# Two transformer blocks on one core: 17 of 22 gate/up pairs of the first block as seven half-size products

## The chip, the core and the metric

The kernel runs on one core of a Trainium2 chip. TensorE (PE) multiplies matrices into PSUM; VectorE (DVE), ScalarE (ACT) and GpSimd (POOL) do the elementwise work; SyncE (SP) only issues transfers between HBM and SBUF. The engines run side by side, each in its own fixed order, and wait for each other on semaphores. The metric is the device time of one execution in microseconds (us).

## The reference, cut to what matters

Two blocks follow each other: 512 positions, width 1024, all in float32. Each is an attention mix and a gated MLP. The change lies in the MLP of the first block:

```
h = rms_norm(x, ln_pre_ffn)                                # 512 x 1024
f = (silu(h @ w_gate) * (h @ w_up)) @ w_down               # w_gate, w_up: 1024 x 2816
x = x + rms_norm(f, ln_post_ffn)
```

## The kernel before

Activations lie transposed in SBUF, as eight tiles of 128 features by 512 positions, and so do the results. To keep float32 accuracy on TensorE, every operand is held as two numbers of a shorter format, hi (the rounded value) and lo (the rest), and every product takes three matmuls: hi·hi, hi·lo and lo·hi (`mm3`). For a weight, `wunit` loads 512 KB (two half units of 128 x 512), ScalarE writes each half's hi (L164) and VectorE its lo (L167). There are two raw buffers (`raw`, two of them in the pool `wts`), and ten of hi and ten of lo. For an activation `split` does the same (L176 to L181).

In `ffn1`, output rows come in 22 pairs, 128 of gate and 128 of up. Each slab is eight blocks of the contraction times three matmuls of 512 columns, so a pair is 48 of them. The normalisation's factor 1/rms per position, R, is applied behind the product: g·R, silu, u·R, their product, and a split into hi and lo, which `w_down` reads (`post`). The first four slabs run side by side (`beside`) in halves of 256 columns, while VectorE still finishes the last stage of the mix in `post`: x is added up, multiplied by `ln_pre_ffn` and split into `h`. R is made behind that (L234 to L236).

A scheduler with a model of the chip sets the order of the instructions on each engine when the kernel is built. All transfers here stand in SyncE's queue in that order, and one that waits for its buffer holds back those behind it.

Of the kernel before, what the change touches and what calls it, by code (L numbers as in the profile page):

```python
# [21 lines left out]
EPS = 1e-6  # L22
BIG = 1e30
WH = 524
# [5 lines left out]
NW = 10  # L30
# [13 lines left out]
KA2 = 6  # L44
BESIDE = 4
NA2 = 4
SLOTS = dict(h=16, o=14, k=16, z=6, v=8, p=8, t=6, m=8)
# [14 lines left out]
class Builder:  # L62
# [120 lines left out]

    def mm3(self, out, ahi, alo, bhi, blo, start, stop):
        mm = self.nc.tensor.matmul
        mm(out, lhsT=ahi, rhs=bhi, start=start, stop=False)  # L186
        mm(out, lhsT=ahi, rhs=blo, start=False, stop=False)  # L187
        mm(out, lhsT=alo, rhs=bhi, start=False, stop=stop)  # L188

# [230 lines left out]
    def setup(self):  # L420
        nc = self.nc
        self.res = None
        self.special = []
        self.mark = None
# [15 lines left out]

    def load_x(self, ks=range(KD)):
        x = []
        for k in ks:
            t = self.slot("v")
            self.load_late(t, self.io["x"][k])
            x.append(t)
        return x
# [89 lines left out]
    def pool_branch(self, us, oT):  # L537
        nc = self.nc
        io = self.io
        add = ALU.add  # L540
        hi, lo = self.wunit("w_pool", 0, 1)[0]
# [6 lines left out]
        for i in range(2):  # L548
            u = us[i]
# [14 lines left out]
            oT[i] = self.split(ps, self.col("pool_scale", i), tag="k")  # L564

    def post(self, a, order, wname, gname, nname, rows):
        nc = self.nc
# [19 lines left out]
        if x is None:  # L587
            x = self.load_x()
        self.res = x
        h = self.h_tiles()  # L590
        gate = None
# [23 lines left out]

    def h_tiles(self):
        return [(self.slot("h", F32R), self.slot("h", F32R)) for _ in range(KD)]

# [10 lines left out]
    def ffn1(self, h, R):  # L629
        nc = self.nc  # L630
        self.tables("silu_and_others")
        get = self.units("w_gu1")
        act = []
        for i in range(KF):
            if i == 0:
# [18 lines left out]
        return self.post(act, None, "w_down", "ln_post_ffn", "ln_mix_2", False)  # L654

    def mix2(self, h, rc):
# [418 lines left out]
```

## Time and profile before

| | |
|---|---|
| median of 3 runs (lowest to highest) | 1339.58 us (1339.52 to 1343.4) |
| the profiled execution | 1343.58 us, span 1341.5 us |
| PE, DVE, ACT, POOL busy, share of the span | 98%, 63%, 50%, 11% |
| mean granted TensorE clock | 0.994 |

The span runs from the first to the last instruction. Busy time is the time in which an engine has an instruction in it. Matmuls overlap in their pipeline: one that "lasts" 0.4 us is followed by the next after 0.23 us, so what it costs is read from the distance of starts. The same holds for VectorE and ScalarE, to a smaller degree.

### The profile page before, as it was taken

The page shows a single profiled execution, that of the slowest core. Times are in us where ns is not written, and L with a number is a line of the kernel's source. Part 1 is how long each engine was busy: PE and PEld are TensorE (multiplying, and loading weights), DVE is VectorE, ACT ScalarE, POOL GpSimd, SP SyncE. Part 2 cuts the span into 40 slices and gives each one's busy share as a digit, 9 for nine tenths or more (in the row PEclk, how much of TensorE's full clock was granted, in tenths as well). Part 3 has the DMA queues.
Part 4 walks back from the last instruction along what each step waited for, and adds up shares of the span by engine and source line. Part 5 has one row for each costly group of instructions (what it writes and reads, how often), then busy time and mean ns, then how long its engine had stood idle before and what let it go on. Part 6 is the DMA issues. An engine that isn't in the chain of part 4 may idle for free.

```text
span 1341.5 us, 20064 instructions
## 1 busy us (share of the span) xinstructions
PE 1311.8 (98%) x7450; PEld 1138.0 (85%) x7450; DVE 851.3 (63%) x1771; ACT 672.6 (50%) x1327; POOL 153.8 (11%) x190
## 2 busy tenths in 40 slices
PE   9799999999999999999999999899999999999998
PEld 9799988988888888888988999779888888888887
DVE  7777885864444432229588878766877777733354
ACT  6466755543333332237576777755554444522241
POOL 1232220000000000001222334430000000000000
PEclk9999999999999999999999999999999999999999
DMA  6322334233333333228244445333332332332221
GB/s 228 109 67 68 95 111 126 70 117 96 96 95 95 94 95 94 95 70 262 88 112 117 123 117 138 93 106 124 126 95 95 94 95 94 102 95 94 94 79 63
DMA packets 48801, 141.69 MB, mean 106 GB/s; under 512 B 6240, under 2 KB 7136, under 8 KB 48704
## 3 DMA queue, kind: packets, MB, share of 16 engines
q1 hardware_dynamic: 48704, 140.42, 34.0%
q8 instruction: 58, 0.95, 0.3%
q14 instruction: 39, 0.32, 0.1%
HBM read 122.38 MB, written 6.29 MB: 96 GB/s over the span
## 4 chain that ended last, share of the span: by engine, by line
PE 84%; DVE 8%; DMA 3%; ACT 2%; issue 2%; SPq 1%; POOL 0%; DVEq 0%; ACTq 0%; POOLq 0%
PE p L186 21%; PE p L187 21%; PE p L188 21%; PE p L372 4%; PE p L373 4%; PE p L374 4%; DVE wl L167 2%; PE p L283 2%; PE p L292 1%; PE p L291 1%; PE p L261 1%; DVE sp L265 1%; PE p L262 1%; DMA wr<-in_w_qk 1%; ACT sp L112 1%
## 5 line engine op out<-in xcount | busy, mean ns | idle before, releaser
L164 ACT ACTIVATE wh<-wr 128x512 fp32r<-128x512 f32 x417 | 259.2, 630 | 405.4 <-PE p L187 351.9
L167 DVE TENSOR_TENSOR wl<-wr,wh 128x512 fp32r<-128x512 f32 (+1 forms) x400 | 286.2, 723 | 238.5 <-ACT wh L164 227.1
L188 PE MATMUL p<-sh,wl 128*128 128x512 f32 (+1 forms) x858 | 320.4, 377 | 0.0
L187 PE MATMUL p<-sh,wh 128*128 128x512 f32 (+1 forms) x858 | 319.5, 376 | 0.1
L186 PE MATMUL p<-sh,wh 128*128 128x512 f32 (+1 forms) x858 | 311.0, 375 | 1.0 <-ACT sh L179 0.7
L372 PE MATMUL p<-wh,sh 128*128 128x256 f32 (+1 forms) x672 | 193.3, 289 | 5.8 <-ACT sz L485 3.3
L373 PE MATMUL p<-wl,sh 128*128 128x256 f32 (+1 forms) x672 | 192.1, 287 | 0.3 <-DVE wl L167 0.2
L374 PE MATMUL p<-wh,sh 128*128 128x256 f32 (+1 forms) x672 | 191.2, 286 | 0.0
L187 PEld LDWEIGHTS p<-sh,wh 128*128 128x128 f32 x858 | 161.2, 188 | 32.6 <-issue 0.5
L188 PEld LDWEIGHTS p<-sh,wl 128*128 128x128 f32 x858 | 161.2, 188 | 31.8 <-issue 0.7
L186 PEld LDWEIGHTS p<-sh,wh 128*128 128x128 f32 x858 | 157.2, 188 | 33.4 <-ACT sh L179 1.1
L372 PEld LDWEIGHTS p<-wh,sh 128*128 128x128 f32 x672 | 128.7, 192 | 9.1 <-ACT sz L485 3.6
L373 PEld LDWEIGHTS p<-wl,sh 128*128 128x128 f32 x672 | 128.9, 192 | 1.1 <-DVE wl L167 0.8
L374 PEld LDWEIGHTS p<-wh,sh 128*128 128x128 f32 x672 | 128.6, 192 | 1.1 <-issue 0.5
L273 POOL TENSOR_SCALAR sp<-sp,m 128x128 f32<-128x128 f32 (+1 forms) x112 | 72.0, 647 | 186.3 <-DVE m L269 145.5
L112 ACT ACTIVATE sp<-sp,m 128x128 f32<-128x128 f32 (+3 forms) x128 | 71.5, 560 | 36.4 <-DVE m L265 33.8
L188 PE MATMUL p<-so,wl 128*128 128x512 f32 (+1 forms) x246 | 88.5, 360 | 0.0
L187 PE MATMUL p<-so,wh 128*128 128x512 f32 (+1 forms) x246 | 88.5, 360 | 0.0
L186 PE MATMUL p<-so,wh 128*128 128x512 f32 (+1 forms) x246 | 87.6, 361 | 0.6 <-DVE m L265 0.5
L167 POOL TENSOR_TENSOR wl<-wr,wh 128x512 fp32r<-128x512 f32 (+1 forms) x17 | 23.8, 1402 | 455.3 <-ACT wh L164 443.7
L265 DVE CUSTOM_DVE_ANT_0 sp<-p,sm 128x128 f32<-128x128 f32 (+3 forms) x128 | 60.4, 483 | 17.3 <-PE p L262 13.5
L187 PE MATMUL p<-sk,wh 128*128 128x512 f32 (+1 forms) x184 | 67.1, 365 | 0.0
(205 smaller groups left out, 2138.8 us busy)
## 6 DMA issues: line engine op xcount, KB each, us to landing
wr<-in_w_gu SPq DMA_DIRECT2D x88, 512.0 KB
wr<-in_w_down SPq DMA_DIRECT2D x44, 512.0 KB
wr<-in_w_qk SPq DMA_DIRECT2D x31, 512.0 KB
sk<-sk SPq DMA_DIRECT2D x88, 128.0 KB
wr<-in_w_out SPq DMA_DIRECT2D x12, 512.0 KB
sv<-in_x SPq DMA_DIRECT2D x16, 256.0 KB
wr<-in_w_ple_gate SPq DMA_DIRECT2D x8, 512.0 KB
wr<-in_w_v SPq DMA_DIRECT2D x6, 512.0 KB
```

What stands on the lines that cost most here:

```text
L112: i = self.nc.scalar.activation(out, in_, func, **k)
L164: nc.scalar.activation(hi[:, :w], c, AF.Copy)
L167: eng.tensor_tensor(lo[:, :w], c, hi[:, :w].bitcast(F32), ALU.subtract)
L186: mm(out, lhsT=ahi, rhs=bhi, start=start, stop=False)
L187: mm(out, lhsT=ahi, rhs=blo, start=False, stop=False)
L188: mm(out, lhsT=alo, rhs=bhi, start=False, stop=stop)
L265: nc.vector.tensor_tensor_reduce(p[:, :n], ps[:, :n], tab[:, (3 - qb) * P:S], 1.0, 3e38, ALU.add, ALU.min, accum_out=m[:, 0:1])
L273: self.nc.gpsimd.tensor_scalar(p[:, :n], p[:, :n], m[:, 2:3], 1.0, ALU.mult, ALU.mult)
L283: ins = nc.tensor.transpose(pt[:, w:w + P], ps_list[qb][:, kb * P:kb * P + P], self.ident)
L372: mm(d, lhsT=h[k][0][:, a], rhs=hi[:, c], start=k == 0 and (o == 0 or not first), stop=False)
L373: mm(d, lhsT=h[k][0][:, a], rhs=lo[:, c], start=False, stop=False)
L374: mm(d, lhsT=h[k][1][:, a], rhs=hi[:, c], start=False, stop=k == 7 and (o > 0 or not first))
```

## The change

Five pairs stay as they were. For the 17 others, the product is cut into blocks: the weights of a pair into gate and up (128 outputs each) by the first and second half of the contraction, the activation into the two halves of the contraction by two halves of the positions. A plain product of two such 2 x 2 block matrices takes eight block products; in the new form (one level of Strassen) it takes seven, with sums of blocks as operands. Each block product is four blocks of the contraction times three matmuls of 256 columns, so a pair is 84 of them.

- The activation's seven operands (28 tiles of hi and lo) are made once: `h_forms` multiplies x by `ln_pre_ffn` and R (`normed`, 16 instructions of 128 x 256), adds and subtracts quarters (8 instructions of 128 x 512) and splits (14 pairs of instructions). The scheduler is given them between the first five pairs. R is now in the operands, not behind the product.
- The weights' seven operands are made for each pair in `w_forms`: both units of the pair are loaded at once, four sums are formed on VectorE, and each of the seven operands is split into hi (ScalarE) and lo (VectorE). The two raw buffers and the numbers of hi and lo buffers are the same.
- Three PSUM tiles A, B, C take the seven products of a pair. Products 5 and 6 run behind the start of the next pair. Copies, additions, silu and multiplications work on 256 columns.
- To free slots, x goes to a tensor in HBM (`parked`, eight stores of 256 KB), and is loaded back for `post`; `act`, `h` and the pool branch's output use other slots.

```diff
     def ffn1(self, h, R):
...
+        self.parked = self.dp.tile([KD, P, S], F32, tag="parked", name="parked")
+        for m in range(KD):
+            nc.sync.dma_start(self.parked[m], self.res[m])
         act = []
-        for i in range(KF):
+        todo = []
+        for i in range(PLAIN):
...
-            act.append(self.split(t, **self.act_tiles(i)))
+            act.append(self.split(t, **self.act_tiles1(i)))
+            if i == 0:
+                forms, todo = self.h_forms(R)
+                each = -(-len(todo) // (PLAIN - 2))
+            else:
+                for step in todo[(i - 1) * each:i * each]:
+                    step()
+        self.res = None
+        sums = [self.slot("m") for _ in range(4)]
+        late = []
+        for i in range(PLAIN, KF):
+            wf = self.w_forms(2 * i, sums)
+            A, B, C = (self.psum(True) for _ in range(3))
+            half = slice(0, 256)
+            e, f, t = self.slot("z"), self.slot("z"), self.slot("z")
+
+            def times(out, j, first=False, wf=wf):
+                hi, lo = wf(j)
+                for k in range(4):
+                    c = slice(k * P, k * P + P)
+                    a = slice(k % 2 * 256, k % 2 * 256 + 256)
+                    bh, bl = forms[j][k // 2]
+                    self.mm3(out[:, half], hi[:, c], lo[:, c], bh[:, a], bl[:, a], first and k == 0, k == 3, True)
+
+            times(A, 0, True)
+            nc.scalar.activation(e[:, half], A[:, half], AF.Copy)
+            times(C, 1, True)
+            for step in late[:1]:
+                step()
+            times(A, 2)
+            nc.scalar.activation(e[:, 256:], A[:, half], AF.Copy)
+            for step in late[1:]:
+                step()
+            times(B, 3, True)
+            nc.vector.tensor_tensor(t[:, half], B[:, half], e[:, half], ALU.add)
+            self.act(t[:, half], t[:, half], AF.Silu)
+            times(A, 4)
+            nc.scalar.activation(f[:, half], A[:, half], AF.Copy)
+            nc.vector.tensor_tensor(f[:, 256:], C[:, half], f[:, half], ALU.add)
+
+            def left(A=A, t=t, times=times):
+                times(A, 5)
+                nc.vector.tensor_tensor(t[:, half], t[:, half], A[:, half], ALU.mult)
+
+            def right(C=C, t=t, e=e, f=f, times=times, i=i):
+                times(C, 6)
+                nc.vector.tensor_tensor(t[:, 256:], C[:, half], e[:, 256:], ALU.add)
+                self.act(t[:, 256:], t[:, 256:], AF.Silu)
+                nc.vector.tensor_tensor(t[:, 256:], t[:, 256:], f[:, 256:], ALU.mult)
+                act.append(self.split(t, -1.0, **self.act_tiles1(i)))
+            late = [left, right]
+        for step in late:
+            step()
...
+    def h_forms(self, R):
...
+        def form(j, src, scale=None):
+            for s in src:
+                hi, lo = (self.slot(tags.pop(0), F32R) for _ in range(2))
+                self.split(s, scale, hi, lo)
+                forms[j].append((hi, lo))
+
+        def normed(a, b):
+            out = [self.slot("o") for _ in range(2)]
+            for k in range(4):
+                m = 4 * a + k
+                c = slice(256 * b, 256 * b + 256)
+                nc.vector.scalar_tensor_tensor(
+                    out[k // 2][:, k % 2 * 256:k % 2 * 256 + 256], x[m][:, c], self.col("ln_pre_ffn", m),
+                    R[:, c], ALU.mult, ALU.mult)
+            quarter[a, b] = out
...
+        sub, add = ALU.subtract, ALU.add
+        return forms, [
+            lambda: normed(0, 0), lambda: normed(0, 1), lambda: form(0, quarter[0, 0]),
+            lambda: keep(1, sub, (0, 0), (0, 1)), lambda: form(1, quarter[1]),
+            lambda: normed(1, 1), lambda: keep(2, add, (1, 1), 1), lambda: form(2, quarter[2], -1.0),
+            lambda: keep(3, sub, (1, 1), (0, 1)), lambda: form(4, quarter[3]),
+            lambda: form(6, quarter[1, 1]), lambda: normed(1, 0), lambda: form(3, quarter[1, 0]),
+            lambda: keep(4, sub, 2, (1, 0)), lambda: form(5, quarter[4])]
+
+    def w_forms(self, u, sums):
+        nc = self.nc
+        raw = []
+        for j in (u, u + 1):
+            t = self.wp.tile([P, 2 * WH], F32, tag="raw", name=self.nm("wr"))
+            nc.sync.dma_start(t[:, :KD * P], self.io["w_gu1"][j])
+            raw += [t[:, 0:512], t[:, 512:1024]]
+        g1, g2, u1, u2 = raw
+        s1, s2, s3, s4 = sums
+        made = {}
...
+        src = [lambda: g1, lambda: plus(s1, u1, u2), lambda: plus(s2, s1, g1), lambda: g2,
+               lambda: plus(s3, g1, u1), lambda: u2, lambda: plus(s4, s2, g2)]
+        for j, f in enumerate(src):
+            c = f()
+            hi = self.wp.tile([P, WH], F32R, tag="hi", name=self.nm("wh"), bufs=NW)
+            lo = self.wp.tile([P, WH], F32R, tag="lo", name=self.nm("wl"), bufs=NW)
+            nc.scalar.activation(hi[:, :512], c, AF.Copy)
+            nc.vector.tensor_tensor(lo[:, :512], c, hi[:, :512].bitcast(F32), ALU.subtract)
+            made[j] = (hi, lo)
+        return made.get
```

The lines of the changed kernel that the order names: L774 a sum of weights, L783 the lo of a weight operand, L738 `normed`, L747 the sums of quarters, L178 and L181 the lo of a split, L654 to L658 the plain pairs' ends; L693 the first silu's input, L697 f's sum, L701 and L705 the reads of products 5 and 6, L707 the last multiplication.

VectorE in the steady part of gate and up, before: in a pair it subtracts four lo (L167), and reads the pair's two sums where they are due (L647, L650).

```order
L647 TENSOR_TENSOR sz_3832<-p_3762,sm_3176 128x512
L167 TENSOR_TENSOR wl_3965<-wr_3958,wh_3964 128x512
L167 TENSOR_TENSOR wl_4006<-wr_4003,wh_4005 128x512
L650 TENSOR_TENSOR sz_3835<-p_3797,sm_3176 128x512
L167 TENSOR_TENSOR wl_4010<-wr_4003,wh_4009 128x512
L651 TENSOR_TENSOR sz_3832<-sz_3832,sz_3835 128x512
L177 TENSOR_TENSOR sk_3839<-sz_3832,sk_3838 128x512
```

The same place now, from the first use of a pair's second raw buffer (wr_4041) to the last; wr_4039 is its first, sm_3787 to sm_3790 are the sums.

```order
L774 TENSOR_TENSOR sm_3787<-wr_4041 128x512
L774 TENSOR_TENSOR sm_3789<-wr_4039,wr_4041 128x512
L697 TENSOR_TENSOR sz_3939<-p_3937,sz_3939 128x256
L774 TENSOR_TENSOR sm_3788<-sm_3787,wr_4039 128x512
L783 TENSOR_TENSOR wl_4049<-sm_3787,wh_4048 128x512
L774 TENSOR_TENSOR sm_3790<-sm_3788,wr_4039 128x512
L701 TENSOR_TENSOR sz_3940<-sz_3940,p_3935 128x256
L783 TENSOR_TENSOR wl_4054<-sm_3788,wh_4053 128x512
L783 TENSOR_TENSOR wl_4058<-wr_4039,wh_4057 128x512
L783 TENSOR_TENSOR wl_4063<-sm_3789,wh_4062 128x512
L705 TENSOR_TENSOR sz_3940<-p_3937,sz_3938 128x256
L783 TENSOR_TENSOR wl_4067<-wr_4041,wh_4066 128x512
```

Twelve instructions lie between the landing of a pair's second load and the release of its buffer; before there were two lo for a buffer. Behind them come one lo, L707, L693, a split's lo and the next pair's first lo.

VectorE at the passage from the plain pairs to the new form: the first sum of weights stands 48th behind R, the lo of product 1 61st, that of product 2 66th. The end of that piece reads:

```order
L178 TENSOR_TENSOR sv_3692<-so_3682,sv_3691 128x512
L178 TENSOR_TENSOR sp_3670<-sz_3663,sp_3669 128x512
L774 TENSOR_TENSOR sm_3788<-sm_3787,wr_3791 128x512
L774 TENSOR_TENSOR sm_3789<-wr_3791,wr_3793 128x512
L783 TENSOR_TENSOR wl_3801<-sm_3787,wh_3800 128x512
L178 TENSOR_TENSOR sv_3700<-so_3695,sv_3699 128x512
L658 TENSOR_TENSOR sz_3777<-sz_3777,sz_3780 128x512
L178 TENSOR_TENSOR sv_3704<-so_3697,sv_3703 128x512
L774 TENSOR_TENSOR sm_3790<-sm_3788,wr_3791 128x512
L783 TENSOR_TENSOR wl_3806<-sm_3788,wh_3805 128x512
```

The activation's operands (L178, and L738, L747 ahead of them) stand in front of the first pair's weight operands, since one engine makes both.

## Rows read from the trace of the kernel before

**Rows 1.** The page: span, and busy time of each engine.

```profile
span 1341.5 us, 20064 instructions
PE 1311.8 (98%) x7450; PEld 1138.0 (85%) x7450; DVE 851.3 (63%) x1771; ACT 672.6 (50%) x1327; POOL 153.8 (11%) x190
```

**Rows 2.** The page: the chain of waits that ended last, by engine.

```profile
PE 84%; DVE 8%; DMA 3%; ACT 2%; issue 2%; SPq 1%; POOL 0%; DVEq 0%; ACTq 0%; POOLq 0%
```

**Rows 3.** Busy time by stretch: us from the start, length, engines with instructions, clock, DMA.

```profile
core 0: us, PE busy (x) PEld busy (x) DVE busy (x) ACT busy (x) POOL busy (x), PEclk, DMA share, GB/s
30.00:40.00 10.00, 10.00 (x87) 10.00 (x86) 9.22 (x14) 3.77 (x8) 6.80 (x7) 1.00 0.50 144
50.00:60.00 10.00, 7.70 (x52) 7.53 (x51) 3.70 (x8) 1.75 (x4) 0.00 (x0) 0.83 0.36 101
168.00:231.00 63.00, 62.48 (x362) 53.96 (x361) 43.95 (x97) 35.28 (x76) 8.45 (x9) 1.00 0.37 115
267.80:292.40 24.60, 24.60 (x108) 19.98 (x107) 17.31 (x28) 11.56 (x21) 0.00 (x0) 1.00 0.39 126
292.43:481.52 189.09, 189.09 (x817) 153.49 (x816) 89.17 (x138) 65.87 (x105) 0.00 (x0) 1.00 0.31 95
```

**Rows 4.** Waits in 292.43 to 481.52 us: who for whom, us, times, longest.

```profile
ACT wh L164 <- PE p L187: 95.0, 51, 2.2
```

**Rows 5.** Timeline of TensorE: start, length, engine, line, operation, tiles, sizes.

```profile
251.94 0.29 PE L188 MATMUL p<-sh,wl 128*128 128x256 f32 x1
252.06 0.28 PE L187 MATMUL p<-sh,wh 128*128 128x256 f32 x1
...
447.02 0.40 PE L188 MATMUL p<-sh,wl 128*128 128x512 f32 x1
447.02 0.19 PEld L186 LDWEIGHTS p<-sh,wh 128*128 128x128 f32 x1
447.25 0.40 PE L186 MATMUL p<-sh,wh 128*128 128x512 f32 x1
```

**Rows 6.** Timeline of VectorE.

```profile
238.46 0.48 DVE L180 SCALAR_TENSOR_TENSOR sh<-sv,cols,sh 128x256 fp32r<-128x256 f32 x1
238.85 0.42 DVE L601 TENSOR_TENSOR sm<-sm,sz 128x256 f32<-128x256 f32 x1
239.19 0.42 DVE L604 TENSOR_TENSOR sv<-sv,sm 128x256 f32<-128x256 f32 x1
...
266.38 0.69 DVE L235 SCALAR_TENSOR_TENSOR sz<-sz,sm 128x512 f32<-128x512 f32 x1
267.11 0.69 DVE L236 SCALAR_TENSOR_TENSOR sm<-sz,sm 128x512 f32<-128x512 f32 x1
...
292.43 0.69 DVE L650 TENSOR_TENSOR sz<-p,sm 128x512 f32<-128x512 f32 x1 [1.60 <-PE p L188]
303.56 0.69 DVE L650 TENSOR_TENSOR sz<-p,sm 128x512 f32<-128x512 f32 x1 [1.64 <-PE p L188]
304.16 0.68 DVE L167 TENSOR_TENSOR wl<-wr,wh 128x512 fp32r<-128x512 f32 x1
...
481.52 0.69 DVE L650 TENSOR_TENSOR sz<-p,sm 128x512 f32<-128x512 f32 x1 [1.46 <-PE p L188]
```

**Rows 7.** Timeline of SyncE's loads, and of the ScalarE instructions that read them.

```profile
264.09 0.33 SPq L158 DMA_DIRECT2D wr<-in_w_gu  x1
265.77 0.33 SPq L158 DMA_DIRECT2D wr<-in_w_gu  x1
267.68 1.16 ACT L164 ACTIVATE wh<-wr 128x512 fp32r<-128x512 f32 x2 [0.85 <-DMA wr<-in_w_gu]
270.31 0.64 ACT L164 ACTIVATE wh<-wr 128x512 fp32r<-128x512 f32 x1 [1.47 <-DVE sz L650]
304.87 0.33 SPq L158 DMA_DIRECT2D wr<-in_w_gu  x1
```

**Rows 8.** Timeline of TensorE in the first stage: a matmul behind a wait.

```profile
54.15 0.30 PE L261 MATMUL p<-sk,sk 128*128 128x128 f32 x1 [2.30 <-DMA sk<-sk]
```

More of the change, by code (lines that the diff above doesn't have):

```diff
@@ L45 @@
 BESIDE = 4
+PLAIN = 5
 NA2 = 4
@@ L182, in split, with mm3 @@
         return hi, lo
-    def mm3(self, out, ahi, alo, bhi, blo, start, stop):
+    def mm3(self, out, ahi, alo, bhi, blo, start, stop, open_group=False):
         mm = self.nc.tensor.matmul
-        mm(out, lhsT=ahi, rhs=bhi, start=start, stop=False)
-        mm(out, lhsT=ahi, rhs=blo, start=False, stop=False)
-        mm(out, lhsT=alo, rhs=bhi, start=False, stop=stop)
+        more = dict(skip_group_check=True) if open_group else {}
+        mm(out, lhsT=ahi, rhs=bhi, start=start, stop=False, **more)
+        mm(out, lhsT=ahi, rhs=blo, start=False, stop=False, **more)
+        mm(out, lhsT=alo, rhs=bhi, start=False, stop=stop, **more)
     def slab(self, out, name, s, h, order=None, halves=((0, S),), units=None, gate=None, free=0):
@@ L422, in setup @@
         self.res = None
+        self.parked = None
         self.special = []
@@ L439, in setup, with load_x @@
         nc.gpsimd.memset(self.one, 1.0)
-    def load_x(self, ks=range(KD)):
+    def load_x(self, ks=range(KD), src=None):
         x = []
@@ L444, in load_x @@
             t = self.slot("v")
[L445 removed]
+            self.load_late(t, (self.io["x"] if src is None else src)[k])
             x.append(t)
@@ L563, in pool_branch @@
             self.mm3(ps, hi[:, c], lo[:, c], dh, dl, True, True)
-            oT[i] = self.split(ps, self.col("pool_scale", i), tag="k")
+            oT[i] = self.split(ps, self.col("pool_scale", i), tag="h")
     def post(self, a, order, wname, gname, nname, rows):
@@ L587, in post @@
         if x is None:
-            x = self.load_x()
+            x = self.load_x(src=self.parked)
         self.res = x
-        h = self.h_tiles()
+        h = self.h_tiles("k" if rows else "h")
         gate = None
@@ L614, in post, with h_tiles @@
         return h, self.rstd_cols(side)
-    def h_tiles(self):
-        return [(self.slot("h", F32R), self.slot("h", F32R)) for _ in range(KD)]
+    def h_tiles(self, tag="h"):
+        return [(self.slot(tag, F32R), self.slot(tag, F32R)) for _ in range(KD)]
     def stats(self, rows, tag="z"):
@@ L653, in ffn1, with act_tiles1, pair, keep @@
+        for step in late:
+            step()
         self.tables("natural_log_exp_and_others")
         return self.post(act, None, "w_down", "ln_post_ffn", "ln_mix_2", False)
+    def act_tiles1(self, i):
+        tag = ("p" * 4 + "t" * 3 + "o" * 7 + "k" * 8)[i]
+        return dict(hi=self.slot(tag, F32R), lo=self.slot(tag, F32R))
+    def h_forms(self, R):
+        nc = self.nc
+        x = self.res
+        tags = ["h"] * 16 + ["m"] * 4 + ["v"] * 8
+        forms = [[], [], [], [], [], [], []]
+        todo = []
+        quarter = {}
+        def form(j, src, scale=None):
[12 more added lines that the diff above has]
+            quarter[a, b] = out
+        def pair(op, p, q):
+            out = []
+            for u, v in zip(p, q):
+                t = self.slot("o")
+                nc.vector.tensor_tensor(t, u, v, op)
+                out.append(t)
+            return out
+        def keep(name, op, p, q):
+            quarter[name] = pair(op, quarter[p], quarter[q])
+        sub, add = ALU.subtract, ALU.add
[6 more added lines that the diff above has]
+            lambda: keep(4, sub, 2, (1, 0)), lambda: form(5, quarter[4])]
@@ new lines, in w_forms, with plus @@
+    def w_forms(self, u, sums):
+        nc = self.nc
+        raw = []
[6 more added lines that the diff above has]
+        made = {}
+        def plus(out, a, b):
+            nc.vector.tensor_tensor(out, a, b, ALU.add)
+            return out
+        src = [lambda: g1, lambda: plus(s1, u1, u2), lambda: plus(s2, s1, g1), lambda: g2,
[8 more added lines that the diff above has]
+        return made.get
```

## The prediction, made blind

> **What bounds the kernel now.** I read the busy times first, then the chain of waits, then the stretch that the change rewrites, and last the distances of starts on TensorE, VectorE and the load queue. TensorE is busy for 98% of the span and VectorE for 63% [rows 1]; 84% of the chain that ended last is TensorE's own work [rows 2]. In the 17 pairs that change, from 292.43 us (the fifth pair's last sum is read) to 481.52 us (the last pair's is) [rows 6], TensorE has no idle time at all: 189.09 us for 17 pairs of 48 matmuls, which is 11.12 us a pair, at full clock, 2.4 GHz (1.00) [rows 3]. The others wait for it: ScalarE's hi has 51 waits for TensorE to give a buffer back, up to 2.2 us each [rows 4]. VectorE is busy for 89.17 us of that stretch, 5.2 us a pair [rows 3]. So less TensorE work saves time there, until VectorE, ScalarE or the loads are late.
>
> **TensorE's part.** Half-size products must not cost more per column. In the stage's first slabs two matmuls of 256 columns start 0.12 us apart [rows 5]; where only 256-column matmuls run, 87 start in 10 us, 0.115 each [rows 3]. I take 0.118. A full one takes 0.23 [rows 5] (189.09 / 816 = 0.232). A pair falls from 11.12 to 84 x 0.118 = 9.91 us, 1.42 us a product; 17 pairs save 20.6 us if nothing is late.
>
> One rule speaks against this. The row shows a weight load of 0.19 us beside a matmul, and 256-column matmuls 0.12 us apart, so loads overlap with each other's work [rows 5]. The Trainium skill, "TensorE: Matmul & The Clock Gate", section "LDWEIGHTS (loading the stationary operand)", has the load's time depend on the stationary columns, not on how many are then streamed, so that halves need twice the loads for the same stream. Its figure of about 107 ns for 128 columns would, as an estimate, still hide under a 256-column stream. What unhidden loads would cost is the last rival.
>
> **VectorE and ScalarE in steady state.** Starts on VectorE lie 0.60 us apart for 128 x 512 (303.56 to 304.16), 0.34 for 128 x 256 and 0.39 with a column factor; with a scalar at 512 I take 0.66, between 0.60 and the 0.73 of two dependent ones [rows 6]. A new pair has four sums, seven lo (11 x 0.60 = 6.6), five instructions of 256 columns (1.7) and a split's lo (0.66): 9.0 us. ScalarE has eight of 512 columns at about 0.53 (two in 1.16 [rows 7]) and five smaller ones, under 7 us. Both fit beside 9.91, VectorE with 0.9 to spare.
>
> **The loads are late instead.** Both raw buffers now belong to one pair. The second is read first by the first sum and last by the lo of product 5; only then may the next pair's load into it be issued. Between stand four sums and lo 1 to 4 (8 x 0.60 = 4.8), three of 256 columns (1.0), and lo 5, which ends 0.69 after its start: 6.5 us. From that end to the issue it is 0.03 us (304.16 + 0.68 to 304.87) [rows 6, 7]. Then the load: one alone, issued at 264.09, is read at 267.68, so 3.59; one issued 1.68 us behind another, at 265.77, is read at 270.31, so at most 4.54 [rows 7]. Here the second follows the first by lo 4, L705 and lo 5, about 1.54 us, so I take 4.45, with 3.59 and 4.54 as ends. The loop is 6.5 + 0.03 + 4.45 = 10.98 us a pair, against 11.12 before: of 1.21 us only 0.14 is left. VectorE then idles some 2 us a pair, waiting for the load, and TensorE 1.07.
>
> **The passage to the new form.** The operands need R, which is there at 267.11 + 0.69 = 267.80 us [rows 6]. TensorE is through the five plain pairs at 292.4, and through product 0 at 293.8. Behind R the order has 61 VectorE instructions up to the lo of product 1: 16 `normed` (6.2), two with a scalar (1.3) and 43 others (25.8), 33.3 us, so it is ready near 301.2. Five more give the lo of product 2 at 304.2. TensorE waits 7.4 us for the one and 1.6 for the other (product 1 ends at 302.6): 9 us. VectorE has 17.3 us of work in 267.8 to 292.4 before [rows 3], so there was little room for 16 x 0.39 + 8 x 0.60 + 12 x 0.60 + 2 x 0.66 = 19.6 us more.
>
> **The sum for gate and up.** Lo 5 of the first new pair ends at 306.1 (three more of 0.60, and latency); the next pair's second load is there at 310.6. The last pair's, 15 loops later, at 475.3. Its lo 1 comes 2.83 us behind (478.1), lo 2 at 479.7; products 2 to 6 take 7.1, so TensorE ends at 486.8 instead of 481.5: +5.3 us. The same from the other side: 9 + 15 x 1.07 + 0.8 (the first loop) - 20.6 = +5.3.
>
> **The rest.** (1) A TensorE that stood still for 2.30 us [rows 8] shows 0.83 in that 10 us stretch [rows 3], so part of it at 1.2 GHz, a loss of 1.7 us. Here it stands for 7.4: I add 1.5, between 0 and twice 1.7. (2) The scheduler moved matmuls in two other places, where the pool branch takes `h` slots and in the second mix's output. TensorE idles 0.5 us in 168 to 231 [rows 3], so no more than that can be won there; a new wait might cost the 2.3 of rows 8 at each. I take 1 us each, 2 in all, with -0.5 and +4.6 as ends. (3) Parking x: eight stores of 256 KB stand in SyncE's queue ahead of the last plain loads, and eight loads among those of `w_down`. The load queue moves data for 0.31 of the time in this stage [rows 3], and each weight load of `w_down` feeds 24 matmuls, 24 x 0.232 = 5.6 us of TensorE, which covers its 3.6. I take nothing; if a parked load holds one back, up to 5.6. (4) Silu, copies and multiplications on 256 columns are in VectorE's and ScalarE's sums above.
>
> 5.3 + 1.5 + 2 = 8.8 us. The profiled execution, 1343.58 us with a span of 1341.5, would be 1352.4; against the median of the runs shown, 1339.58, it is 1348.4 us. A change under 0.3%, 4 us, can't be told from none here.
>
> **Rivals.**
> - *Faster: the second load lands like one alone.* The decisive point is whether it takes 3.59 or 4.45. For it speaks that the transfer engines are busy for 0.31 of the time [rows 3]; against it, the 4.54 of the one row with two loads so close [rows 7]. The loop is 10.12 us, the last pair's load is there at 309.7 + 15 x 10.12 = 461.5, TensorE ends at 473.0, 8.5 us early; with 3.5 for the rest, 1334.6 us. Chance 0.08.
> - *Slower still: VectorE waits inside the loop.* L701, L705 and L697 read products or ScalarE's copies in the middle of the loop, and VectorE can't pass them. If they cost 0.5 us a pair together, 15 loops add 7.8: 1356.2 us. For it speaks that TensorE, itself late, feeds them; against it, that its products need 9.91 of the 10.98. Chance 0.22.
> - *No change: the passage is hidden.* If the operands were ready when TensorE arrives, all loops start 9 us earlier: 1339.4 us. For it: VectorE idles 7.3 of 24.6 us there before [rows 3]; against: the 61 instructions. Chance 0.10.
> - *Much slower: loads of weights don't hide at 256 columns.* A product would take the load's 0.19 [rows 5]: 84 x 0.19 = 16.0 us a pair, 17 x 4.84 = 82 us more, 1430 us with the rest. Against it stands the 0.12 of the same shape in the same stage. Chance 0.02.
>
> **How the numbers follow.** The forecast has 0.58, with its own range of 1343 to 1355 (loop 10.8 to 11.1, the clock and the moved matmuls at their ends). The range of 1337 to 1360 leaves out most of the faster rival, the last one and the far ends. Faster by over 0.3% (under 1335.6): 0.08. Within: the hidden passage and the forecast's lower edge, 0.15. Slower: 0.77.
>
> **What would show it.** In the new profile, matmuls of 256 columns start 0.118 us apart; the gate/up loads come in twos, 10.98 us from pair to pair; the first sum (L774) waits for a load once a pair, for about 1 us or more; TensorE idles about 1 us a pair, before the first matmuls of product 0 or 1; near 293 to 304 us it idles 9 us. Loads 10.1 us apart, or L774 never waiting for one, would make the forecast wrong; so would a passage with TensorE busy.

## The result, and the profile after

The changed kernel takes 1350.86 us (median of 8 runs, 1344.21 to 1353.09), against 1340.24 us for the kernel before in the same session (8 runs, 1339.52 to 1346.39). The ratio is 1.0061, 95% interval 1.0038 to 1.0084: slower. The profiled execution took 1350.33 us with a span of 1348.5, 7.0 us more than the span before.

The page of the changed kernel: span, busy time of each engine, and the chain of waits that ended last by engine and by line.

```profile
span 1348.5 us, 21638 instructions
PE 1302.2 (97%) x8062; PEld 1156.7 (86%) x8062; DVE 937.3 (70%) x1962; ACT 724.0 (54%) x1460; POOL 153.5 (11%) x190
PE 69%; DVE 20%; DMA 7%; issue 2%; ACT 2%; SPq 0%; POOL 0%; DVEq 0%; ACTq 0%; POOLq 0%
PE p L188 16%; PE p L190 16%; PE p L189 16%; DMA wr<-in_w_gu 5%; PE p L374 5%; PE p L375 5%; PE p L376 4%; DVE wl L783 4%; DVE sm L774 3%; DVE wl L168 2%; PE p L285 2%; PE p L294 1%; PE p L293 1%; PE p L263 1%; DVE sp L267 1%
```

Against [rows 1, 2] TensorE has 9.6 us less work, and yet the span is longer. Its share of the chain fell from 84% to 69%; VectorE's rose from 8% to 20% and that of the transfers from 3% to 7%, and the lines that stand for most of this are those of the new form: the gate/up loads (5%), the lo of the weight operands (L783, 4%) and the sums (L774, 3%). What bounds this stage has changed hands.

Busy time by stretch in the changed kernel, with the columns of [rows 3]. The stretches are one ahead of the MLP, the one in which the operands are made, the passage, and a steady part of the new pairs.

```profile
core 0: us, PE busy (x) PEld busy (x) DVE busy (x) ACT busy (x) POOL busy (x), PEclk, DMA share, GB/s
190.00:200.00 10.00, 8.31 (x38) 6.57 (x37) 7.45 (x16) 2.69 (x5) 0.00 (x0) 0.86 0.34 112
272.20:295.00 22.80, 22.80 (x100) 18.50 (x100) 22.80 (x44) 11.71 (x19) 0.00 (x0) 1.00 0.07 26
295.00:309.90 14.90, 8.01 (x40) 7.07 (x39) 14.90 (x27) 7.29 (x13) 0.00 (x0) 0.66 0.01 4
320.00:440.00 120.00, 114.58 (x928) 110.97 (x927) 100.86 (x188) 69.17 (x143) 0.00 (x0) 0.99 0.30 97
```

Two places show idle time on a TensorE that had none in [rows 3]. In the passage (third row) it is busy for 8.0 of 14.9 us, while VectorE has no idle time at all, from 272.2 to 309.9. In the steady part, 928 matmuls start in 120 us. A pair is 84 of them, so a pair takes 84 x 120 / 928 = 10.86 us; the loads, whose second one of a pair is issued 15 times from 309.96 to 471.63, say 161.67 / 15 = 10.78. Before, it was 11.12. The half products themselves keep their pace, 0.12 us from start to start (296.87 to 296.99 below) as in [rows 5]. TensorE's idle time is 5.4 of the 120 us, some 0.5 us a pair, while a pair takes 0.95 to 1.05 us longer than one without waits: a matmul that lasts 0.28 us still runs when the next could have started, 0.12 us behind it, so short pauses do not show as idle, which may be where the rest lies.

**The passage.** TensorE's timeline (start, length, line, sizes, and in brackets the idle time before and what ended it). L188 is hi times hi, L190 the one that needs a lo of the weights.

```profile
296.87 0.28 PE L189 MATMUL p<-sh,wh 128*128 128x256 f32 x1
296.99 0.28 PE L190 MATMUL p<-sh,wl 128*128 128x256 f32 x1
299.36 0.39 PE L188 MATMUL p<-sh,wh 128*128 128x256 f32 x1 [2.09 <-ACT wh L782]
299.58 0.32 PE L189 MATMUL p<-sh,wh 128*128 128x256 f32 x1
304.63 0.58 PE L188 MATMUL p<-sh,wh 128*128 128x256 f32 x1 [4.73 <-ACT wh L782]
305.01 0.42 PE L189 MATMUL p<-sh,wh 128*128 128x256 f32 x1
305.23 0.53 PE L190 MATMUL p<-sh,wl 128*128 128x256 f32 x1
305.55 0.41 PE L188 MATMUL p<-sh,wh 128*128 128x256 f32 x1
...
307.69 0.41 PE L189 MATMUL p<-sv,wh 128*128 128x256 f32 x1
308.18 0.58 PE L190 MATMUL p<-sh,wl 128*128 128x256 f32 x1
...
309.84 0.33 PE L188 MATMUL p<-sh,wh 128*128 128x256 f32 x1
310.00 0.28 PE L189 MATMUL p<-sh,wh 128*128 128x256 f32 x1
```

VectorE's timeline in the same stretch: the lo of products 1 and 2 of the first new pair.

```profile
304.43 0.69 DVE L783 TENSOR_TENSOR wl<-sm,wh 128x512 fp32r<-128x512 f32 x1
...
307.44 0.68 DVE L783 TENSOR_TENSOR wl<-sm,wh 128x512 fp32r<-128x512 f32 x1
```

Product 0 is through at 297.3. Of products 1 and 2 only matmuls that need no lo can start (299.36 to 305.01); the first with a lo starts at 305.23, 0.11 us behind the end of that lo (304.43 + 0.69), and the next such pair of rows is 308.12 and 308.18. So it is VectorE's queue that TensorE waits for, although the rows name ScalarE's hi: the hi that ends the 4.73 us is that of product 2, which waits for a sum (L774) in the same queue. The hi that ends the 2.09 us comes from ScalarE's own queue (its sum is ready at 297.29), but product 1 could not have gone on without its lo in any case. From 299.4 to 309.8 most starts lie 0.21 us apart, not 0.12, and the granted clock from 299.0 to 309.8 is 0.53: TensorE runs almost all of it at 1.2 GHz, and the 0.66 is the mean of the longer window. From 296.99 to 310.00 lie 25 starts, worth 25 x 0.118 = 2.95 us at full clock; the passage costs 13.01 - 2.95 = 10.06 us.

**The loop.** SyncE's gate/up loads (two for each pair) and VectorE's first and last use of the second raw buffer in one pair.

```profile
329.86 0.33 SPq L767 DMA_DIRECT2D wr<-in_w_gu  x1
331.39 0.33 SPq L767 DMA_DIRECT2D wr<-in_w_gu  x1
...
340.08 0.33 SPq L767 DMA_DIRECT2D wr<-in_w_gu  x1
341.61 0.33 SPq L767 DMA_DIRECT2D wr<-in_w_gu  x1
```

```profile
335.08 0.69 DVE L774 TENSOR_TENSOR sm<-wr 128x512 f32<-128x512 f32 x1 [0.22 <-DMA wr<-in_w_gu]
...
340.90 0.68 DVE L783 TENSOR_TENSOR wl<-wr,wh 128x512 fp32r<-128x512 f32 x1
```

The second load is issued at 331.39 and read at 335.08 (3.69 us); from there to the end of lo 5 at 341.58 it is 6.50 us, and 0.03 later the next one is issued: 10.22 us. In other loops the load takes longer, up to 4.64 us; the mean of the loop is 10.78. VectorE's waits from 320 to 470 us (who for whom: us in total, times, longest) tell that the loads end the largest part of its idle time in the steady part, 10.0 of some 22 us.

```profile
DVE sm L774 <- DMA wr<-in_w_gu: 10.0, 12, 1.3
DVE sz L693 <- PE p L190: 5.9, 8, 1.6
DVE wl L783 <- ACT wh L782: 3.4, 5, 1.2
```

**Where the 7.0 us arise.** Starts of one and the same instruction or load in both timelines:

| | before | after | shift |
|---|---|---|---|
| VectorE reads the first plain pair's product | 268.96 | 272.25 | +3.3 |
| first load of `in_p` behind the MLP | 571.65 | 578.75 | +7.1 |
| first load of `in_w_out2a` | 795.33 | 800.66 | +5.3 |
| first load of `in_w_ple_gate` | 1258.41 | 1265.47 | +7.1 |
| end of the span | 1341.5 | 1348.5 | +7.0 |

So 3.3 us are lost ahead of the MLP, 3.8 between there and `in_p`, and behind that it comes out even.

### The profile page after: what moved, and what is told of

It reads as the page before. It is cut to its first block, busy times and chain, and to the rows that moved or that the text cites. A ratio compares the mean times of both kernels' runs of the same rounds, so it can differ in the third digit from the quotient of the medians.

```text
span 1348.5 us, 21638 instructions
## 1 busy us (share of the span) xinstructions
PE 1302.2 (97%) x8062; PEld 1156.7 (86%) x8062; DVE 937.3 (70%) x1962; ACT 724.0 (54%) x1460; POOL 153.5 (11%) x190
## 4 chain that ended last, share of the span: by engine, by line
PE 69%; DVE 20%; DMA 7%; issue 2%; ACT 2%; SPq 0%; POOL 0%; DVEq 0%; ACTq 0%; POOLq 0%
PE p L188 16%; PE p L190 16%; PE p L189 16%; DMA wr<-in_w_gu 5%; PE p L374 5%; PE p L375 5%; PE p L376 4%; DVE wl L783 4%; DVE sm L774 3%; DVE wl L168 2%; PE p L285 2%; PE p L294 1%; PE p L293 1%; PE p L263 1%; DVE sp L267 1%
## 5 line engine op out<-in xcount | busy, mean ns | idle before, releaser
L168 DVE TENSOR_TENSOR wl<-wr,wh 128x512 fp32r<-128x512 f32 x332 | 237.4, 727 | 200.6 <-ACT wh L165 193.3
L165 ACT ACTIVATE wh<-wr 128x512 fp32r<-128x512 f32 (+1 forms) x349 | 215.8, 629 | 294.4 <-PE p L189 237.6
L188 PE MATMUL p<-sh,wh 128*128 128x512 f32 (+1 forms) x768 | 260.3, 343 | 10.7 <-ACT wh L782 10.1
L190 PE MATMUL p<-sh,wl 128*128 128x512 f32 (+1 forms) x768 | 263.9, 345 | 2.9 <-DVE wl L783 2.4
L189 PE MATMUL p<-sh,wh 128*128 128x512 f32 (+1 forms) x768 | 261.3, 342 | 0.0
L188 PEld LDWEIGHTS p<-sh,wh 128*128 128x128 f32 x768 | 144.3, 189 | 31.1 <-ACT wh L782 12.5
L190 PEld LDWEIGHTS p<-sh,wl 128*128 128x128 f32 x768 | 145.7, 190 | 24.4 <-DVE wl L783 6.4
L189 PEld LDWEIGHTS p<-sh,wh 128*128 128x128 f32 x768 | 145.6, 190 | 18.2 <-issue 0.2
L189 PE MATMUL p<-sk,wh 128*128 128x512 f32 (+1 forms) x274 | 95.1, 354 | 0.1
L190 PE MATMUL p<-sk,wl 128*128 128x512 f32 (+1 forms) x274 | 95.2, 354 | 0.0
L188 PE MATMUL p<-sk,wh 128*128 128x512 f32 (+1 forms) x274 | 88.3, 354 | 1.9 <-ACT sk L177 1.4
L188 PE MATMUL p<-so,wh 128*128 128x512 f32 (+1 forms) x246 | 88.5, 364 | 0.6 <-DVE m L267 0.5
L190 PE MATMUL p<-so,wl 128*128 128x512 f32 (+1 forms) x246 | 88.9, 362 | 0.0
```

The source lines that it names most:

```text
L165: nc.scalar.activation(hi[:, :w], c, AF.Copy)
L168: eng.tensor_tensor(lo[:, :w], c, hi[:, :w].bitcast(F32), ALU.subtract)
L188: mm(out, lhsT=ahi, rhs=bhi, start=start, stop=False, **more)
L189: mm(out, lhsT=ahi, rhs=blo, start=False, stop=False, **more)
L190: mm(out, lhsT=alo, rhs=bhi, start=False, stop=stop, **more)
```

## The experiments

Medians stand beside the kernel before, run in between on the same chip; of each profile I read the steady part from 320 or 330 to 440 us (us of a pair = 84 times the stretch over its matmuls) and TensorE's waits near 300 us. Where lines are added above them, L774 and L783 have other numbers.

Falls against the changed kernel (1350.86 us) compare runs of different sessions, between which the median of the kernel before moved from 1340.24 to 1342.45 us; differences of 1 to 2 us between such falls show nothing.

**One load for a pair.** Up's unit is not loaded, and gate's data stands for it; the instructions on the engines are the same in number.

```diff
-        for j in (u, u + 1):
-            t = self.wp.tile([P, 2 * WH], F32, tag="raw", name=self.nm("wr"))
-            nc.sync.dma_start(t[:, :KD * P], self.io["w_gu1"][j])
-            raw += [t[:, 0:512], t[:, 512:1024]]
+        t = self.wp.tile([P, 2 * WH], F32, tag="raw", name=self.nm("wr"))
+        nc.sync.dma_start(t[:, :KD * P], self.io["w_gu1"][u])
+        raw += [t[:, 0:512], t[:, 512:1024]] * 2
```

> The second unit of each of the 17 pairs is not loaded: gate's data serves as up's too, so up's result is left out. VectorE, ScalarE and TensorE do what they did; a pair needs one raw buffer, and the two buffers alternate. Theory (the loop load - release - load sets the pace): the pair falls from 10.78 us to TensorE's 9.9 to 10.1, 15 loops x 0.7 to 0.9 = 10 to 13 us less, 1338 to 1341 us. Rival (VectorE's work and its waits inside its own queue set the pace): VectorE's queue is the same, the pair stays at 10.8 us and the time at 1350 us, within 2. Second rival (TensorE's half-size matmuls set it): 1350 us as well.

Measured: 1335.4 us (1332.7 to 1336.79), ratio to before 0.995 [0.9933, 0.9967]. Its steady part, with the columns of the stretches above:

```profile
320.00:440.00 120.00, 120.00 (x1025) 120.00 (x1024) 114.90 (x215) 77.61 (x160) 0.00 (x0) 1.00 0.17 55
```

TensorE has no idle time, a pair takes 84 x 120 / 1025 = 9.83 us, and VectorE waits for no load there. With all its work it is busy for 114.9 of 120 us. So it was the loads that held the pairs at 10.8, and VectorE's work does fit, barely. The time came out 3 us under the range expected. The waits of the passage are unchanged, 2 of 6.8 us together, the longest 4.7.

**Sums on GpSimd.** If VectorE's load of work were the limit, giving four sums of 0.60 us to an idle engine would help.

```diff
         def plus(out, a, b):
-            nc.vector.tensor_tensor(out, a, b, ALU.add)
+            nc.gpsimd.tensor_tensor(out, a, b, ALU.add)
```

> The four sums of weights of each pair go from VectorE to GpSimd, where a 128x512 subtraction takes 1.40 us instead of 0.60. VectorE's work falls from 9.0 to 6.6 us a pair. Rival (VectorE's work sets the pace): the pair falls to TensorE's 9.9, 13 us less, 1338 us. Theory (the loop through the raw buffers): the second buffer is now read by sums of 1.4 us each, and lo 2 waits for the third of them; the way from its landing to its release grows from 6.5 to 7.5 to 9 us, the pair to 11.8 to 13.3 us, 15 to 38 us more, 1366 to 1389 us.

Measured: 1384.68 us, ratio 1.032 [1.0302, 1.0337]; a pair takes 84 x 110 / 731 = 12.64 us. The groups of lo instructions and sums from 320 to 490 us (busy us, mean ns of one, idle time before and what ended it), in this kernel:

```profile
L783 DVE TENSOR_TENSOR wl<-sm,wh 128x512 fp32r<-128x512 f32 x55 | 49.9, 907 | 32.8 <-ACT wh L782 32.8
L774 POOL TENSOR_TENSOR sm<-sm,wr 128x512 f32<-128x512 f32 x26 | 39.3, 1511 | 1.0
```

a piece of the timelines of VectorE and of GpSimd,

```profile
330.36 1.12 DVE L783 TENSOR_TENSOR wl<-sm,wh 128x512 fp32r<-128x512 f32 x1 [1.24 <-ACT wh L782]
331.40 0.41 DVE L705 TENSOR_TENSOR sz<-p,sz 128x256 f32<-128x256 f32 x1
```

```profile
329.62 1.31 POOL L774 TENSOR_TENSOR sm<-wr,wr 128x512 f32<-128x512 f32 x1
330.88 1.75 POOL L774 TENSOR_TENSOR sm<-sm,wr 128x512 f32<-128x512 f32 x1
```

and in the changed kernel:

```profile
L783 DVE TENSOR_TENSOR wl<-sm,wh 128x512 fp32r<-128x512 f32 x61 | 41.8, 685 | 0.0
```

A sum takes 1.3 to 1.5 us in place of 0.68, the sums follow each other, and the mean of the lo rises from 685 to 907 ns; the one at 330.36, beside sums, takes 1.12 us. The chain from the landing to the release got longer, which costs time by the loop's theory; but lo instructions that take longer would also cost time if VectorE were the limit. So the size of the loss alone does not separate the two. VectorE's busy time does speak against the second: it is 69.3 of the 110 us from 330 to 440. And GpSimd is no cheap helper here.

**Release early.** The four sums come first, then the operands that are read from a raw buffer itself; instructions and buffers are the same.

```diff
-        for j, f in enumerate(src):
-            c = f()
+        src = [f() for f in (src[0], src[1], src[4], src[2], src[6], src[3], src[5])]
+        src = dict(zip((0, 1, 4, 2, 6, 3, 5), src))
+        for j in (0, 5, 3, 1, 2, 4, 6):
+            c = src[j]
```

> Only the order in which the weight operands are made is changed: the four sums first, then the operands 0, 5 and 3 that read the raw buffers, then 1, 2, 4 and 6, which read sums. Same work on every engine, same buffers. Theory (loop through the raw buffers): they are given back behind four sums and three lo, 4.2 us, and what stands between them, instead of 6.5; the loop is under 9.9 us, TensorE sets the pace, 15 x 0.8 = 12 to 14 us less, 1336 to 1339 us. Rival (VectorE's work or TensorE): 1350 us, within 2.

Measured: 1331.89 us (1331.19 to 1332.55), ratio 0.9927 [0.9912, 0.9941]. Its steady part, and VectorE's wait for the loads from 320 to 440 us:

```profile
320.00:440.00 120.00, 120.00 (x1027) 120.00 (x1026) 114.39 (x214) 77.84 (x163) 0.00 (x0) 1.00 0.35 115
```

```profile
DVE sm L774 <- DMA wr<-in_w_gu: 0.4, 1, 0.4
```

The same loads of the same size now cost nothing: a pair takes 9.81 us. Not the transfer as such but the time for which a pair holds its buffers was the limit. From 10.86 to 9.81 it is 1.05 us a pair, 17.9 us over 17; the median falls by 19.0 against the changed kernel, 4 us more than the range expected allowed. Part of the difference is the passage, where TensorE's waits fall from 7.7 to 5.8 us in all (290 to 345 us).

**Seven plain pairs.** `PLAIN = 5` becomes 7: 15 pairs in the new form, and two plain pairs more, over which the activation's operands can be made.

```diff
-PLAIN = 5
+PLAIN = 7
```

> Seven plain pairs instead of five, the other 15 in the new form. VectorE has two pairs more (22 us, some 12 of them free) to make the activation's operands. Theory (the passage costs 9 us of waiting and the lower clock behind it): the wait of TensorE near 300 us is gone or under 2 us, the clock stays at 2.4 GHz there; two pairs at 11.12 instead of 10.78 cost 0.7; 8 to 11 us less, 1339 to 1343 us. Rival (the wait there belongs to the first loads into the two raw buffers, not to the operands): it moves along with the passage, 1350 us, within 2.

Measured: 1339.86 us (10 runs, 1336.57 to 1346.21), ratio 0.999 [0.9975, 1.0005]. The stretch of the passage in this kernel, two pairs later than in the changed one:

```profile
315.00:330.00 15.00, 14.53 (x110) 13.72 (x109) 11.44 (x21) 7.43 (x16) 0.00 (x0) 1.00 0.21 71
```

The first half product starts at 318.05, the lo of product 1 is ready at 315.2, and the clock stays at 1.00; from 300 to 345 us TensorE waits once, for 0.5 us. The pairs still take 84 x 120 / 949 = 10.62. So the passage's price goes when the operands have time (10.06 us above; the median falls by 11.0 against the changed kernel), and the loop's doesn't; two pairs fewer in the new form cost nothing as long as such a pair saves next to nothing.

**Operands on GpSimd.** The other way to shorten the passage: twelve of the fourteen lo of the activation's operands on GpSimd.

```diff
-                self.split(s, scale, hi, lo)
+                if j in (0, 1, 4, 6, 3, 5):
+                    nc.scalar.activation(hi, s, AF.Copy)
+                    nc.gpsimd.tensor_tensor(lo, s, hi.bitcast(F32), ALU.subtract)
+                else:
+                    self.split(s, scale, hi, lo)
```

> Of the activation's 14 lo, the 12 without a scale are made on GpSimd (1.4 us each, idle there) instead of VectorE (0.60); the pairs are as in the changed kernel. Theory (the passage waits because VectorE has 61 instructions to do ahead of the first new operand): VectorE has 12 x 0.60 = 7.2 us less there, the wait of TensorE near 300 us falls from 9 us to 1 to 3, and with it most of the time at the lower clock; the pairs stay at 10.8 us. 6 to 10 us less, 1341 to 1345 us. Rival (the wait there is for the loads of the first weights): no change, 1350 us, within 2.

Measured: 1354.4 us, ratio 1.0092 [1.0077, 1.0107]: a miss, since it got slower than the changed kernel. TensorE's waits from 290 to 320 us rise from 6.8 to 11.5 us. Why is in VectorE's rows. `normed` as a group from 262 to 320 us, and two timelines, of VectorE and of GpSimd:

```profile
L742 DVE SCALAR_TENSOR_TENSOR so<-sv,cols,sm 128x256 f32<-128x256 f32 x16 | 14.8, 990 | 0.0
```

```profile
282.78 4.77 DVE L742 SCALAR_TENSOR_TENSOR so<-sv,cols,sm 128x256 f32<-128x256 f32 x4
```

```profile
283.00 2.83 POOL L732 TENSOR_TENSOR sh<-so,sh 128x512 fp32r<-128x512 f32 x2 [5.63 <-ACT sh L731]
```

and the same group in the changed kernel:

```profile
L738 DVE SCALAR_TENSOR_TENSOR so<-sv,cols,sm 128x256 f32<-128x256 f32 x16 | 6.8, 481 | 0.0
```

One `normed` takes 990 ns in the mean in place of 481, and four of them fill 4.8 us just where GpSimd has two subtractions of 1.4 us. The 16 take 8 us more, which is more than the 7.2 us that the twelve lo would have saved. The Trainium skill, "SBUF — State Buffer", section "Who interferes with whom", has VectorE and GpSimd share a pair of ports under an exclusive lock, and names a VectorE instruction with two inputs in SBUF against a GpSimd instruction that reads SBUF. The trace agrees: `normed` reads two tiles in SBUF and doubles. In the kernel with the sums on GpSimd, the lo at 330.36, which reads two, takes 1.12 us, while L705 at 331.40, which reads one operand from PSUM, keeps its 0.41 beside a sum (0.42 in the changed kernel).

**Three edits together:** early release, the lo of the operands on GpSimd, and six plain pairs (`PLAIN = 6`).

> Release in the new order, 12 lo on GpSimd, and six plain pairs together. Theory (two separate losses, the loop and the passage): pairs at 9.8 us as with the release alone (1331.9 us), no wait at the passage (6 to 10 us less), one pair fewer in the new form (1.2 us more): 1323 to 1327 us. Rival (one of them only hid the other; with the pairs at 9.8 us VectorE, at 9.0 us a pair, has no time to catch up and gives the gain back): 1330 us or more.

Measured: 1330.85 us (1328.82 to 1333.77), ratio 0.9918 [0.99, 0.9936]. A miss of some 4 us, in the range that the rival had: the pairs are at 84 x 110 / 941 = 9.82, but TensorE still waits up to 312 us, for a lo of L783's kind (2 times, 6.1 us, the longest 5.5).

**Four raw buffers.** `bufs=4` for the raw tiles wherever weights are loaded, and `NW`, the number of hi and lo buffers, 8 in place of 10 for the room.

```diff
-NW = 10
+NW = 8
...
-            t = self.wp.tile([P, 2 * WH], F32, tag="raw", name=self.nm("wr"))
+            t = self.wp.tile([P, 2 * WH], F32, tag="raw", name=self.nm("wr"), bufs=4)
```

> Four raw buffers instead of two, paid with eight hi and lo buffers instead of ten (for all stages); the order of the operands is the changed kernel's. Theory (loop through two raw buffers): a pair's loads can land while the pair before is made; pairs at TensorE's 9.8 to 9.9 us, 15 x 0.9 = 13 us less, plus or minus 3 for the fewer hi and lo buffers: 1334 to 1340 us. Rival (the operands' order is what matters, not the buffers): 1350 us, within 3.

Measured: 1327.72 us (1324.16 to 1329.39), ratio 0.9889 [0.9869, 0.9909]. Its steady part:

```profile
320.00:440.00 120.00, 120.00 (x1028) 120.00 (x1027) 115.08 (x215) 77.10 (x160) 0.00 (x0) 1.00 0.34 111
```

The pairs are at 84 x 120 / 1028 = 9.81, VectorE has no wait for a load from 320 to 470 us, and the passage's waits are still there (7.5 us). That is the loop's theory again, from the side of the buffers. It is faster than I had expected, because four buffers also change the rest of the kernel; the control below sizes that.

**Four raw buffers, with the lo of the operands on GpSimd and six plain pairs,** the edits shown above put together.

> Four raw buffers with eight hi and lo, 12 lo on GpSimd, six plain pairs. Theory: the loop is broken by buffers instead of by the order, the passage as before: 1322 to 1328 us, the same as with the early release within 3. Rival (eight hi and lo buffers are too few for seven operands a pair, of which two are held into the next pair): pairs of 10.3 us or more, 1330 us or more.

Measured: 1327.14 us, ratio 0.9891 [0.9874, 0.9907], no different from the run above, and 3.7 us under the three edits with the early release; the passage keeps two waits for the lo of the weights, 5.4 us together.

**The control: the kernel before with four raw buffers** and `NW = 8`, without any half product.

> The kernel before, with all 22 pairs plain, and with four raw buffers and eight hi and lo as in e7. It tells how much of e7's 1327.7 us belongs to the half-size products. Theory (the plain pairs never wait for a load; TensorE idles not at all there): pairs stay at 11.12 us; what e7 won outside gate and up (about 9 us of its 23, after that stage) comes from the buffers and shows here too: 1330 to 1336 us. Rival (the buffers only serve the new form): 1340 to 1343 us, like the kernel before.

Measured: 1334.73 us (1333.64 to 1337.96), ratio 0.9947 [0.993, 0.9964]. So some 0.5% of the 1.1 to 1.4% that the kernels with four buffers win belongs to the buffers alone. It does not arise in gate and up: there VectorE first reads a pair's product at 272.26 us in place of 268.96 and last at 483.37 in place of 481.52, while the span ends at 1336.2 in place of 1341.5.

**Four raw buffers and seven plain pairs.** The edits shown above, against both of the changed kernel's losses at once.

> e7 with seven plain pairs; no operand on GpSimd. Theory (the passage costs 9 us and the lower clock, and e5 failed only because GpSimd and VectorE stood in each other's way): no wait of TensorE near 300 us, two pairs more at 11.12 instead of 9.6 (3 us): 1319 to 1324 us. Rival (VectorE, with pairs at 9.6 us, has the operands' work only pushed along): 1327 us, within 2.

Measured: 1322.9 us (1321.06 to 1323.56), ratio 0.9859 [0.9845, 0.9874]: the fastest of all. The passage and the steady part:

```profile
315.00:330.00 15.00, 14.47 (x96) 13.04 (x95) 12.76 (x22) 6.16 (x13) 0.00 (x0) 1.00 0.22 70
330.00:440.00 110.00, 110.00 (x940) 110.00 (x939) 105.42 (x196) 71.56 (x149) 0.00 (x0) 1.00 0.34 111
```

TensorE waits once in the first, for 0.5 us, and never in the second. Beside the control in the same session, 15 pairs as half products are worth 1334.73 - 1322.9 = 11.8 us. That is net of a later start: R is ready at 275.3 us here and at 271.1 in the control.

**Early release and seven plain pairs**, the edits shown above, with two raw buffers as in the changed kernel.

> e3 (the order that gives the raw buffers back early) with seven plain pairs, two raw buffers. Theory: as e10 against e7, 4 to 8 us under e3's 1331.9: 1324 to 1328 us. Rival (work pushed along): 1332 us, within 2.

Measured: 1326.05 us (1321.47 to 1326.35), ratio 0.9877 [0.9859, 0.9895]. An order of instructions and one constant, with no more room, turn the loss of 0.6% into a gain of 1.2%.

**Only the pool branch's slot.** The kernel before with the one edit that touches the program ahead of the MLP.

```diff
-            oT[i] = self.split(ps, self.col("pool_scale", i), tag="k")
+            oT[i] = self.split(ps, self.col("pool_scale", i), tag="h")
```

> The kernel before with one change: the pool branch's output goes to slots h instead of k, as in the changed kernel. It tells whether the 3.5 us by which gate and up start later there come from that move. Theory (they do: the scheduler moves matmuls around the pool branch, TensorE waits twice for over 1 us near 194 us and falls to the lower clock): gate and up start 2 to 4 us later, 1342 to 1345 us. Rival (they come from the slots of the norm's operands h or from the stores of x): no later start, 1340 to 1342 us.

Measured: 1343.48 us (10 runs, 1342.09 to 1347.99), ratio 1.0021 [1.0008, 1.0034]. TensorE's timeline and the stretch from 190 to 200 us in this kernel:

```profile
194.76 0.47 PE L291 MATMUL p<-st,sv 128*128 128x512 f32 x1 [1.06 <-DVE so L296]
195.87 0.50 PE L292 MATMUL p<-st,sv 128*128 128x512 f32 x1 [0.64 <-DVE st L177]
```

```profile
190.00:200.00 10.00, 8.31 (x43) 6.63 (x42) 7.33 (x16) 3.11 (x6) 0.00 (x0) 1.00 0.34 116
```

In the changed kernel the same two waits stand at 194.88 and 195.99, 1.06 and 0.64 us again, and TensorE is busy for the same 8.31 of 10 us; before it was 10.00 of 10. The lower clock that I had expected with them is not there. With this slot alone the first plain pair is read 2.2 us later (271.1). The rest of the 3.3 us is within what single executions differ by: in the profiles of the eight kernels with this slot, half products and two raw buffers, TensorE is busy for 8.31 us in that stretch each time, and the first plain pair is read between 269.80 and 272.29 us, 271.1 in the mean. The two with a clock of 1.00 there are read at 269.80 and 270.30, the six with 0.83 to 0.86 at 270.33 to 272.29; that the clock makes this difference was not tested. So the slot costs some 2 us ahead of the MLP. By the end of the span nothing of it is left in the profiled executions (1341.5 us in both), while the medians differ by 2.3.

## Why the prediction was right

The forecast was slower, 1348.4 us in a range of 1337 to 1360; measured were 1350.86. By its steps:

- **TensorE's part** held. A pair on which TensorE never waits takes 9.81 to 9.83 us in three kernels, against 9.91 forecast, and 11.12 before. Loads of weights hide at 256 columns, so the much slower rival is out; they do so although a load lasts 0.19 us in the rows, more than the estimate in the prediction.
- **The load loop** held, and was the decisive step: 10.98 us a pair forecast, 10.78 measured. Its fixed part came out as worked (6.50 + 0.03 us); the second load was read 3.7 to 4.6 us behind its issue, where I had taken 4.45 throughout. One load fewer, an earlier release and two more buffers each bring the pair to 9.8 us, by three different ways to the same buffer. So the faster rival (the second load always like one alone, 10.12 us a pair) is seen in single loops, as in the 10.22 above, and not in the mean. Of VectorE's idle time, which I had at some 2 us a pair and all for the load, the load ends 0.7 of 1.6 us (320 to 470 us). Why some loads are short and others not stays open.
- **VectorE waits inside the loop** (the slower rival, 0.22) is out in the mean: with its loads in time VectorE has 114 to 115 us of work in 120 and TensorE does not wait. In one of the 15 loops it is there: at 371.79 VectorE waits 0.93 us for the product that L701 reads. (This rival's 15 x 0.5 us are 7.5, not 7.8, which changes no verdict.) Its waits for L693 and L783 in the changed kernel follow from a TensorE and a ScalarE that are late themselves.
- **The passage** held in size. I had the lo of products 1 and 2 ready at 301.2 and 304.2; they were at 305.12 and 308.12. Of that, R was 3.4 us late (271.22 in place of 267.80), so the 61 and 66 instructions were sized within some 0.5 us. The two waits that I forecast (7.4 and 1.6) became one stretch of 8.0 us with four matmuls in it (297.3 to 305.2), and the second was filled by a product at 1.2 GHz. With the clock I had 9 + 1.5 = 10.5 us, measured were 10.06.
- **The hidden passage** (no change, 0.10) is out for five plain pairs. With seven it is what happens, and that kernel comes out at no change, 0.999, as this rival had it.
- **The rest** was mis-sized. For the moved matmuls near the pool branch I had 1 us, and the slot costs some 2, the whole step ahead of the MLP 3.3 in the profiled execution. For the second mix I had 1 more; there nothing is left at the end of the span (+7.1 at `in_p`, +7.0 at the end). The parked x cost nothing that shows: TensorE's waits from 309.9 to 471.6 us are all for operands.

The sum for gate and up, +5.3 and +1.5 for the clock, stands against +3.8 measured. Put together from the rows: 10.06 for the passage, 15 loops of 10.78 - 9.83 = 0.95 each make 14.3, some 0.8 for the first loop as forecast (not measured), less 17 x (11.12 - 9.83) = 21.9: +3.2. TensorE's rows say nearly the same: its first matmul of `w_down` stands at 481.32 us before, its last half product now ends at 494.06, with 6.17 us of `w_down` in between, so gate and up end 6.6 us later, 3.3 of them from the later start. The remaining 0.5 us up to `in_p` I did not take apart. That the sum came so near is in part luck: gate and up with the clock were forecast some 3 us too high (the loop 0.20 us too long, 15 times) and the second mix 1 too high, the step ahead of the MLP 2.3 too low. The forecast for the span was +8.8, the profiled spans differ by 7.0, and the medians by 10.6; the execution profiled before lay 3.3 us above its median, and the one after 0.5 below, which is as much as these two differ.

The change is not bad in itself. Its arithmetic saves TensorE 1.29 us a pair, and more than that was lost to the time for which a pair keeps its raw buffers and to one engine that must make all operands while TensorE is already through. With both removed it is worth 11.8 us on top of what the buffers alone bring.

## What to carry to other kernels

An operation that saves TensorE work through sums of operands moves work to the engines that make operands, and lengthens the time for which a loaded tile is held; compute the loop from a buffer's release through its load to its next release, and set it beside the new, shorter time of TensorE. The order within that loop can decide more than its amount of work: using up the raw tiles first was worth some 18 us with the same instructions and buffers. Where a new form needs operands made beforehand, count the instructions of their engine against the old work that is to cover them, and leave more of that: here two pairs more were enough, and one more, with lo on GpSimd, was not.

## What the runs showed of the hardware

- VectorE instructions that read two tiles in SBUF take longer while GpSimd reads SBUF too: `normed` 990 in place of 481 ns in the mean, the lo of weights 907 in place of 685. An instruction with one operand from PSUM (L705) keeps its 0.41 us beside a sum. The same sum takes 1.3 to 1.5 us on GpSimd and 0.68 on VectorE. An idle GpSimd is no free help to a VectorE with such instructions.
- The waits of TensorE in the passage are followed by matmuls at half the clock: 0.21 us from start to start behind 2.09 and 4.73 us of idle time, until 309.8 us, a granted clock of 0.53 in 299 to 309.8. Where the passage has no such waits, the clock there is 1.00 (315 to 330 us with seven plain pairs). Shorter waits did not always do it: behind the same 1.06 and 0.64 us the clock of 190 to 200 us is 0.86 in the changed kernel and 1.00 in the kernel with the pool branch's slot alone. The runs of the changed kernel spread over 8.9 us, those of the best one over 2.5; the mean granted clock is 0.994 in its fastest run and 0.987 in its slowest, but that the clock makes the difference was not tested.
- Four raw buffers in place of two, with two hi and two lo buffers fewer, make the kernel before 0.5% faster, though TensorE was at 98% of the span.
